# Moving the transposed input by 96 bytes in SBUF, in a two-layer hybrid encoder

## The chip, the cores and the metric

The kernel runs on one core of a Trainium2 chip. The metric is the device time of one execution in microseconds (us); before the change its median over three runs is 1843.59 us. The profile of one execution is read beside it. In it PE is TensorE's matmuls, PEld its weight loads (the loading of the stationary operand), DVE is VectorE, ACT ScalarE, POOL GpSimd, and SP the engine that issues most DMAs.

## What is computed

Two encoder layers over x of 512 tokens by 1024 channels, in float32. Each layer has three sub-layers, and each ends with `x = LayerNorm(ALPHA * x + f(x))`:

```python
proj = x @ w_in                       # queries, keys, values of A and B; u, v of C; gate logits
out_a = window_attention(aq, ak, av, a_sink)        # +-128 tokens, rotary, a sink logit per head
out_b = dense_block_attention(bq, bk, bv)           # all tokens, RMS-normed q and k, 2-D rotary
out_c = spatial_gating(u, v, c_ln_g, c_ln_b, c_ws, c_bs)
branches = jnp.stack([out_a, out_b, out_c], axis=2)
gates = jax.nn.sigmoid(gate + b_gate).reshape(B, S, N_BRANCH, D_MODEL)
h = (jnp.einsum('bsnc,ncd->bsnd', branches, w_branch) * gates).sum(axis=2) @ w_mix_out
...
h = memory_cross_attention(x, mem, x_wq, x_wkv, x_wo)   # 4 heads, 256 memory tokens
...
h = conv_ffn(x, f_w_up, f_conv_k, f_conv_b, f_w_down)   # 2 x 2816 channels, 3-tap convolution
```

## The kernel before

**Products in three parts.** Every float32 operand of a projection is kept as two float32r tiles, a high part (`split_hi`, on ACT) and the rest (`split_lo`, on DVE, in four cases on POOL). A product is three matmuls into the same PSUM bank, high by high, high by low and low by high: `mm3`, lines 137 to 140. The profile therefore shows most matmuls under L138, L139 and L140, and one 128-deep step of a product as one of each. In `nc.tensor.matmul(ps, lhsT=..., rhs=...)` `lhsT` is stationary (128 columns of 128 rows) and `rhs` moves (up to 512 columns).

**The transposed input.** `xT` (line 90) holds x transposed, as [128 partitions, 4 token tiles, high or low, 8 channel tiles, 128 tokens], 32 KB of each partition. It is written at the start from a transposed copy of the input (`split_xt`, line 1097), and three times a layer from TensorE transposes (`xT_step`, line 219, with `ident`; not at the end of the last layer). It is read in two forms:

- `proj_tm` (line 202): xT is stationary, one tile of 128 tokens, and a weight of 512 (keys and values: 256) contiguous columns moves. Used by `v_step`, `u_step`, `q_step` and `kv_step`.
- `proj_fm` (line 209): a weight is stationary and xT moves, four blocks of 128 tokens that lie 8 KB apart, or two of them (`hf`). Used by `gate_step`, `wq_step`, `up_step` and, in halves, `up_half_step`.

All other products have neither operand in xT: the branch projections (`br_step`), the mixer output (`mix_step`, operands `mh` and `ml`), the products with the memory (`mk_step`, `mv_step`, operand `memT`), attention, `wo_step` and the down projection (`down_mm`, operand `g`).

**Weights.** `Weights` (line 143) streams 292 chunks of 512 KB in the order in which the steps need them: a DMA on SP into one of two `raw` buffers, then a split into one of six `w` slots. A full step of the up projection uses one chunk in 8 x 3 = 24 matmuls of 512 columns; a step of the down projection uses one chunk in 4 x 2 x 3 = 24.

**Order.** `layer` puts the steps of a layer into a list (from line 943 on): v and u, the queries with the spatial gating between them, keys and values, then the 16 units of attention A between the gates and projections of branch C, attention B between those of branch A, those of branch B, the mixer output, cross attention, the up projection (22 pairs of steps, the first four steps in halves of 256 tokens) and the down projection. TensorE executes in the order that the scheduler makes of this list.

**Memory.** Tiles come from pools that are laid out in the order of their creation, each tile rounded up to 32 bytes. `cpool` (line 78) is the first and holds, in this order, `xT`, `rope`, `btab`, `mask`, `ident`, `ident_r`, `pp`, `hbias` and `mhalf`. In the compiled kernel `xT` starts at byte 1152 of every partition, `ident` at 41600 and `ident_r` at 42112, each a multiple of 128. Behind `cpool` come `wpool` (first `raw` at 44640, first `w` at 52832), `big`, `kv_p` and `sp`; each tile of these four pools starts 96 bytes past a multiple of 128. `mhalf` is one column of -0.5, the exponent in `rstd_of` (line 197).

Of the kernel before, what the change touches and what calls it, by code (L numbers as in the profile page):

```python
# [10 lines left out]
F32 = mybir.dt.float32  # L11
# [5 lines left out]
P = 128  # L17
# [56 lines left out]
def encoder_kernel(ctx: ExitStack, tc: tile.TileContext, x_in, xt_in, mem_in, w_in, pp_in, ln_in, cln_in, ws_in, co_in, out):  # L74
# [3 lines left out]
    cpool = ctx.enter_context(tc.tile_pool(name="cpool", bufs=1))  # L78
# [8 lines left out]
    ps_t = ctx.enter_context(tc.tile_pool(name="ps_t", bufs=2, space=PSUM))  # L87

    X = {}
    xT = cpool.tile([P, NT, 2, KD, P], F32R, name="xT")  # L90
    dram = ctx.enter_context(tc.tile_pool(name="dram", bufs=1, space=bass.MemoryType.DRAM))
    x_keep = dram.tile([S, DM], F32, name="x_keep")
# [4 lines left out]
    ident_r = cpool.tile([P, P], F32R, name="ident_r")  # L97
    pp = cpool.tile([P, PP_N], F32, name="pp")
    hbias = cpool.tile([P, 24], F32, name="hbias")
    mhalf = cpool.tile([P, 1], F32, name="mhalf")  # L100

    def acc_tile(n=512):
        return ps_acc.tile([P, 512], F32, tag="acc", name="acc")
# [16 lines left out]
    def sm(n, name):  # L120
        return small.tile([P, n], F32, tag=name, name=name)
# [17 lines left out]
        nc.tensor.matmul(ps, lhsT=lh, rhs=rl, start=False, stop=False)  # L139
        nc.tensor.matmul(ps, lhsT=ll, rhs=rh, start=False, stop=last)  # L140

# [1 line left out]
    class Weights:  # L143
        def __init__(self):
            self.order, self.pos, self.last = [], {}, []
# [47 lines left out]
    def pump():  # L193
        W.pump(cur[0])

# [1 line left out]
    def rstd_of(var, n, name):  # L197
        r = sm(n, name)
        nc.gpsimd.tensor_tensor(out=r, in0=var, in1=mhalf.to_broadcast([P, n]), op=ALU.pow)  # L199
        return r  # L200
# [14 lines left out]
    def evac_T(dst_h, dst_l, ps):  # L215
        split_hi(dst_h, ps)
        split_lo(dst_l, ps, dst_h)

    def xT_step(t):
        def fn():  # L220
            for i in range(2):
                pt = t_tile()
                for j in range(4):
                    k = 4 * i + j
                    nc.tensor.transpose(pt[:, j, :], X[0][:, t, k * P:(k + 1) * P], ident)
                evac_T(xT[:, t, 0, 4 * i:4 * i + 4, :], xT[:, t, 1, 4 * i:4 * i + 4, :], pt)
# [5 lines left out]
    def residual(t, half, ps):  # L232
        xs = X[0][:, t, half * 512:(half + 1) * 512]
        nc.vector.scalar_tensor_tensor(out=xs, in0=xs, scalar=ALPHA, in1=ps, op0=ALU.mult, op1=ALU.add)  # L234
        if half == 0:
            ln_stats[t] = small.tile([P, 2, 6], F32, tag="bn", name="bn", bufs=4)
        nc.vector.bn_stats(out=ln_stats[t][:, half, :], in_=xs)

    def ln_finish(t, g, b):
# [6 lines left out]
        for hf in range(2):  # L246
            xt = X[0][:, t, hf * 512:hf * 512 + 512]
            nc.vector.scalar_tensor_tensor(out=xt, in0=xt, scalar=mv[:, 0:1], in1=g[hf], op0=ALU.subtract, op1=ALU.mult)
        for hf in range(2):
            xt = X[0][:, t, hf * 512:hf * 512 + 512]  # L250
            nc.vector.scalar_tensor_tensor(out=xt, in0=xt, scalar=rs, in1=b[hf], op0=ALU.mult, op1=ALU.add)
# [11 lines left out]
        return tiles  # L263

    def rope_rot(t1, t2, src, cos, sin, nh, w):
        # rotate-half within blocks of 2*w, on nh heads of 64
        nb = 64 // (2 * w)
        s4 = src.rearrange("p h (b s d) -> p h b s d", b=nb, s=2)
        o4 = t2.rearrange("p h (b s d) -> p h b s d", b=nb, s=2)
        n4 = sin.rearrange("p (b s d) -> p b s d", b=nb, s=2)  # L270
        nc.vector.tensor_tensor(out=t1, in0=src, in1=cos[:, None, :].to_broadcast([P, nh, 64]), op=ALU.mult)
        for s in range(2):
            if nb == 1:
                nc.vector.tensor_tensor(out=o4[:, :, 0, s, :], in0=s4[:, :, 0, 1 - s, :],
                                        in1=n4[:, 0, s, :][:, None, :].to_broadcast([P, nh, w]), op=ALU.mult)
            else:
                nc.vector.tensor_tensor(out=o4[:, :, :, s, :], in0=s4[:, :, :, 1 - s, :],
                                        in1=n4[:, :, s, :][:, None, :, :].to_broadcast([P, nh, nb, w]), op=ALU.mult)
# [6 lines left out]
    def layer(l):  # L285
        K = lambda kind, c: (l, kind, c)
        R = {}
        last_layer = l == NLAYER - 1

# [1 line left out]
        def params():  # L291
            dma = nc.sync if l == 0 else nc.scalar
            dma.dma_start(out=pp, in_=pp_in[l])
            act(hbias, pp[:, PP_GATE:PP_GATE + 24], AF.Copy, scale=0.5)
            cl = kv_p.tile([P, 2, 512], F32, tag="k", name="cln")
            dma.dma_start(out=cl[:, 0, :], in_=cln_in[l, 0].partition_broadcast(P))
            dma.dma_start(out=cl[:, 1, :], in_=cln_in[l, 1].partition_broadcast(P))
            R["cln"] = cl
            wr = p_tile(name="wsraw")
            dma.dma_start(out=wr, in_=ws_in[l])  # L300
            ws = kv_p.tile([P, 2, 4, P], F32R, tag="v", name="ws", bufs=2)
            wr3 = wr.rearrange("p (g i) -> p g i", g=4)
            split_hi(ws[:, 0], wr3)
            split_lo(ws[:, 1], wr3, ws[:, 0])
            R["ws"] = ws
            R["vc"] = big_tile([P, 2, NT, 512], F32R, "vc")
            R["u"] = big_tile([P, NT, 512], F32, "u")
# [9 lines left out]
                nc.gpsimd.tensor_tensor(out=btab[:, i], in0=b4[:, i % 2],  # L317
                                        in1=g[:, None, :].to_broadcast([P, NT, 64]), op=ALU.mult)

# [1 line left out]
        def v_step(t):  # L321
            def fn():
                ps = acc_tile()
# [47 lines left out]
                pump()  # L371
            return Step(fn)

# [1 line left out]
        def q_step(nm, t):  # L375
            chunks = [K(nm + "q", c) for c in range(4)]

# [22 lines left out]
        def rms(src, tmp, nh):  # L400
            act(tmp, src, AF.Square)
            ss = sm(nh, "ss%d" % nh)
            nc.vector.tensor_reduce(out=ss, in_=tmp, axis=AX.X, op=ALU.add)
            nc.vector.tensor_scalar(out=ss, in0=ss, scalar1=1.0 / 64, scalar2=RMS_EPS, op0=ALU.mult, op1=ALU.add)
# [59 lines left out]
                pump()  # L464
            return Step(fn)

# [1 line left out]
        def a_keys(q):  # L468
            return max(0, q - 1), min(NT - 1, q + 1)

# [82 lines left out]
                evac_pv("A", h, ps)  # L553
            return Step(fn, urgent=True)

# [1 line left out]
        def bS_step(u):  # L557
            def fn():
                h, pr = u // 2, u % 2
# [3 lines left out]
                for qi in range(2):  # L563
                    q = 2 * pr + qi
                    ps = s_tile()
                    for hl in range(2):
                        nc.tensor.matmul(ps, lhsT=R["Q"][:, h, q * P:(q + 1) * P], rhs=R["Kt"][:, kv * 2 + hl, :],  # L567
                                         start=hl == 0, stop=hl == 1)
                    nc.vector.tensor_reduce(out=nm[:, qi:qi + 1], in_=ps, axis=AX.X, op=ALU.max, negate=True)  # L569
                    pm = pm_slot(2 * u + qi)  # L570
# [37 lines left out]
                    evac_pv("B", h, R.pop("pv"))  # L608
            return Step(fn, urgent=True)

# [1 line left out]
        def ring():  # L612
            if "ring" not in R:
                R["ring"] = big_tile([P, 8, 512], F32, "ring")
            return R["ring"]

        def pm_slot(i):
            return ring()[:, i % 4, :]
# [55 lines left out]
                f.append(br_step(n, m, stage))  # L674
            return f

# [1 line left out]
        def mix_step(half, t):  # L678
            chunks = [K("mix", half * 4 + c) for c in range(4)]

# [12 lines left out]
                    ln_finish(t, *R["ln"])  # L693
            return Step(fn, chunks)

# [1 line left out]
        def memT_step():  # L697
            def fn():
                R["memT"] = big_tile([P, 2, KD, NMEM], F32R, "memT")
# [138 lines left out]
                ln_finish(t, *R["ln"])  # L838
            return Step(fn, chunks)

# [1 line left out]
        def g_slot(j):  # L842
            if j % 4 == 0 and j < 20:
                R["g", j // 4] = big_tile([P, 4, 2, S], F32R, "g")
            elif j == 20:
                R["g", 5] = kv_p.tile([P, 2, 2, S], F32R, tag="k", name="g5")
            return g_view(j)
# [92 lines left out]
                        nc.sync.dma_start(out=out[t * P:(t + 1) * P, sl], in_=X[0][:, t, sl])  # L940
            return Step(fn, [K("down", 11 + c) for c in cs])

# [1 line left out]
        def st(s):  # L944
            steps.append(s)

# [139 lines left out]
    for l in range(NLAYER):  # L1086
        layer(l)
# [37 lines left out]
            W.pump(i)  # L1125


# [1 line left out]
def _pack_weights(d):  # L1129
    out = np.empty((NLAYER * NCH, P, 1024), np.float32)  # L1130

    def tm(w, c0, n, nk):
        # (K, n) columns c0.. cut in chunks of nk k-tiles: [p, k, n]
        kt = w.shape[0] // P
        a = w[:, c0:c0 + n].reshape(kt // nk, nk, P, n).transpose(0, 2, 1, 3)
        return a.reshape(kt // nk, P, nk * n)

    def fm(w):
        # (K, M) as [m, p, k, 128]
        kt, mt = w.shape[0] // P, w.shape[1] // P  # L1140
        return w.reshape(kt, P, mt, P).transpose(2, 1, 0, 3).reshape(mt, P, kt * P)

    for l in range(NLAYER):
        def put(kind, a):
            i = l * NCH + CHUNK_ID[kind, 0]
            out[i:i + a.shape[0]] = a

        w = d["w_in"][l]
        put("aq", tm(w, 0, 512, 2))
        put("akv", tm(w, 512, 256, 4))  # L1150
        put("bq", tm(w, 768, 512, 2))
        put("bkv", tm(w, 1280, 256, 4))
        put("u", tm(w, 1536, 512, 2))
        put("v", tm(w, 2048, 512, 2))
        put("gate", fm(w[:, 2560:]))
        put("br", np.concatenate([fm(d["w_branch"][l, n]).reshape(4, 2, P, 512).transpose(0, 2, 1, 3).reshape(4, P, 1024)
                                  for n in range(3)]))
        w = d["w_mix_out"][l]
        put("mix", np.concatenate([tm(w, 0, 512, 2), tm(w, 512, 512, 2)]))
        put("wq", fm(d["x_wq"][l]))  # L1160
        w = d["x_wkv"][l]
        put("mk", fm(w[:, :512]))
        put("mv", tm(w, 512, 512, 2))
        w = d["x_wo"][l]
        put("wo", np.concatenate([tm(w, 0, 512, 2), tm(w, 512, 512, 2)]))
        put("up", fm(d["f_w_up"][l]))
        w = d["f_w_down"][l]
        put("down", np.concatenate([tm(w, 0, 512, 2), tm(w, 512, 512, 2)]))
    return out
# [65 lines left out]
```

## Time and profile before

| what | value |
|---|---|
| median of three runs (lowest, highest) | 1843.59 us (1843.54, 1844.64) |
| span of the profiled execution | 1842.8 us |
| mean granted TensorE clock in it | 0.994 of full speed |
| matmuls in the trace | 9064 |

The span runs from the first to the last instruction of the profiled execution; the runs' median is 0.8 us longer. The page lists busy time by engine, the chain of work that ended last, and the costliest groups of instructions. A group's row gives line, engine, operation, out<-in with the moving operand first for matmuls, partitions by elements, the count, then busy time and the mean duration of one. Matmuls overlap each other: one starts before the last one has ended, so the mean duration of one is longer than the distance between two starts. A few matmul records are missing from the trace.

### The profile page before, as it was taken

The page shows a single profiled execution, that of the slowest core. Times are in us where ns is not written, and L with a number is a line of the kernel's source. Part 1 is how long each engine was busy: PE and PEld are TensorE (multiplying, and loading weights), DVE is VectorE, ACT ScalarE, POOL GpSimd, SP SyncE. Part 2 cuts the span into 40 slices and gives each one's busy share as a digit, 9 for nine tenths or more (in the row PEclk, how much of TensorE's full clock was granted, in tenths as well). Part 3 has the DMA queues.
Part 4 walks back from the last instruction along what each step waited for, and adds up shares of the span by engine and source line. Part 5 has one row for each costly group of instructions (what it writes and reads, how often), then busy time and mean ns, then how long its engine had stood idle before and what let it go on. Part 6 is the DMA issues. An engine that isn't in the chain of part 4 may idle for free.

```text
span 1842.8 us, 23541 instructions
## 1 busy us (share of the span) xinstructions
PE 1811.5 (98%) x9064; PEld 1516.5 (82%) x9064; DVE 1065.9 (58%) x1728; ACT 756.0 (41%) x1274; POOL 316.4 (17%) x320
## 2 busy tenths in 40 slices
PE   8999999999999999999999999999999999999998
PEld 6888888878978888888888888888789788888886
DVE  5566856557675555533466568565575755555334
ACT  4346635532534443331133565455325244444210
POOL 1112422220131111100011124331201311111000
PEclk9999999999999999999999999999999999999999
DMA  6221221232413222232233212212333222222321
GB/s 221 88 78 65 81 92 58 71 132 95 150 69 103 92 92 92 99 119 92 92 131 105 79 70 83 79 58 81 129 109 130 81 92 92 92 102 92 103 103 46
DMA packets 51233, 176.60 MB, mean 96 GB/s; under 512 B 5681, under 2 KB 6193, under 8 KB 50865
## 3 DMA queue, kind: packets, MB, share of 16 engines
q1 hardware_dynamic: 44784, 158.86, 24.8%
q10 hardware_dynamic: 6336, 16.23, 2.7%
q8 instruction: 72, 1.18, 0.3%
q14 instruction: 41, 0.33, 0.1%
HBM read 170.87 MB, written 4.19 MB: 95 GB/s over the span
## 4 chain that ended last, share of the span: by engine, by line
PE 97%; DVE 1%; ACT 1%; DMA 0%; issue 0%; DVEq 0%; SPq 0%
PE acc L138 26%; PE acc L139 26%; PE acc L140 26%; PE s L567 2%; PE pv L604 1%; PE t L590 1%; PE s L138 1%; PE s L140 1%; PE s L139 1%; PE t L140 1%; PE t L138 1%; PE t L139 1%; PE pv L139 1%; PE pv L549 1%; PE s L483 1%; PE pv L138 1%
## 5 line engine op out<-in xcount | busy, mean ns | idle before, releaser
L132 DVE TENSOR_TENSOR w<-raw,w 128x1024 fp32r<-128x1024 f32 x284 | 354.8, 1250 | 454.0 <-ACT w L127 452.9
L127 ACT ACTIVATE w<-raw 128x1024 fp32r<-128x1024 f32 x292 | 309.4, 1060 | 495.7 <-PE acc L140 276.7
L138 PE MATMUL acc<-xT,w 128*128 128x512 f32 (+1 forms) x1216 | 463.3, 382 | 4.5 <-DVE x L234 4.2
L140 PE MATMUL acc<-xT,w 128*128 128x512 f32 (+1 forms) x1216 | 464.5, 382 | 0.0
L139 PE MATMUL acc<-xT,w 128*128 128x512 f32 (+1 forms) x1216 | 462.6, 381 | 0.0
L138 PEld LDWEIGHTS acc<-xT,w 128*128 128x128 f32 x1216 | 228.4, 188 | 50.1 <-DVE x L234 4.6
L140 PEld LDWEIGHTS acc<-xT,w 128*128 128x128 f32 x1216 | 229.2, 189 | 45.8
L139 PEld LDWEIGHTS acc<-xT,w 128*128 128x128 f32 x1216 | 229.3, 189 | 45.5
L138 PE MATMUL acc<-w,xT 128*128 128x512 f32 (+1 forms) x384 | 138.2, 362 | 7.4 <-ACT w L127 7.2
L139 PE MATMUL acc<-w,xT 128*128 128x512 f32 (+1 forms) x384 | 138.6, 361 | 1.2 <-DVE w L132 1.2
L140 PE MATMUL acc<-w,xT 128*128 128x512 f32 (+1 forms) x384 | 138.4, 360 | 0.0
L870 POOL TENSOR_TENSOR cv<-cv 128x512 f32<-128x512 f32 x44 | 56.8, 1292 | 445.4 <-DVE cv L858 402.2
L199 POOL TENSOR_TENSOR rs<-ve,mhalf 128x1 f32<-128x1 f32 x32 | 30.2, 942 | 422.4 <-DVE ve L244 371.4
L138 PEld LDWEIGHTS acc<-w,xT 128*128 128x128 f32 x384 | 72.8, 189 | 18.9 <-ACT w L127 7.8
L139 PEld LDWEIGHTS acc<-w,xT 128*128 128x128 f32 x384 | 72.6, 189 | 13.5 <-DVE w L132 2.0
L140 PEld LDWEIGHTS acc<-w,xT 128*128 128x128 f32 x384 | 72.7, 189 | 10.8
L502 POOL TENSOR_SCALAR ring<-ring,rsm 128x256 f32<-128x256 f32 (+1 forms) x64 | 43.6, 693 | 186.2 <-DVE rsm L500 108.3
L569 DVE TENSOR_REDUCE nm<-s 128x1 f32<-128x512 f32 x64 | 43.9, 688 | 54.2 <-PE s L567 53.5
L124 ACT ACTIVATE ring<-s,nm 128x512 f32<-128x512 f32 x64 | 44.0, 688 | 69.7 <-PE t L590 45.4
L655 POOL TENSOR_TENSOR mg<-mg,ring 128x512 f32<-128x512 f32 x32 | 47.8, 1498 | 140.4 <-DVE ring L654 112.4
L576 POOL TENSOR_SCALAR ring<-ring,rsm 128x512 f32<-128x512 f32 x64 | 45.7, 727 | 129.7 <-DVE rsm L574 129.7
L124 ACT ACTIVATE cv<-acc,pp 128x512 f32<-128x512 f32 x86 | 65.4, 760 | 1.5 <-PE acc L140 1.5
(237 smaller groups left out, 3302.7 us busy)
## 6 DMA issues: line engine op xcount, KB each, us to landing
raw<-in_w_dram SPq DMA_DIRECT2D x292, 512.0 KB, 3.5
lngb<-in_ln_dram ACTq DMA_DIRECT2D x16, 256.0 KB, 4.3
xraw<-in_xt_dram SPq DMA_DIRECT2D x4, 512.0 KB, 4.7
memr<-in_mem_dram ACTq DMA_DIRECT2D x2, 1024.0 KB, 4.8
x<-in_x_dram ACTq DMA_DIRECT2D x4, 512.0 KB, 7.3
x_keep<-x ACTq DMA_DIRECT2D x4, 512.0 KB, 2.6
x<-x_keep ACTq DMA_DIRECT2D x4, 512.0 KB, 7.5
out_dram<-x SPq DMA_DIRECT2D x8, 256.0 KB, 2.0
```

The lines of the kernel that those rows point to most:

```text
L124: return nc.scalar.activation(out, in_, func, **kw)
L127: nc.scalar.activation(out, in_, AF.Copy, scale=scale)
L132: eng.tensor_tensor(out=out, in0=in_, in1=hi.bitcast(F32), op=ALU.subtract)
L138: nc.tensor.matmul(ps, lhsT=lh, rhs=rh, start=first, stop=False)
L139: nc.tensor.matmul(ps, lhsT=lh, rhs=rl, start=False, stop=False)
L140: nc.tensor.matmul(ps, lhsT=ll, rhs=rh, start=False, stop=last)
L502: nc.gpsimd.tensor_scalar(out=pr_t[qi], in0=pr_t[qi], scalar1=rs[:, qi:qi + 1], scalar2=0.0, op0=ALU.mult, op1=ALU.add)
L567: nc.tensor.matmul(ps, lhsT=R["Q"][:, h, q * P:(q + 1) * P], rhs=R["Kt"][:, kv * 2 + hl, :], start=hl == 0, stop=hl == 1)
L569: nc.vector.tensor_reduce(out=nm[:, qi:qi + 1], in_=ps, axis=AX.X, op=ALU.max, negate=True)
L576: nc.gpsimd.tensor_scalar(out=pr_t[qi], in0=pr_t[qi], scalar1=rs[:, qi:qi + 1], scalar2=0.0, op0=ALU.mult, op1=ALU.add)
L655: nc.gpsimd.tensor_tensor(out=mg, in0=mg, in1=tg, op=ALU.add)
L870: nc.gpsimd.tensor_tensor(out=c, in0=ca, in1=c, op=ALU.mult)
```

## The change

A tile `lead` of 24 floats (96 bytes) is put ahead of `xT` in `cpool`. `mhalf` is no longer a tile, but the first column of `lead`. Behind `hbias`, where `mhalf` was, stands a tile of 16 floats (64 bytes) that nothing uses.

```diff
     X = {}
+    lead = cpool.tile([P, 24], F32, name="lead")
     xT = cpool.tile([P, NT, 2, KD, P], F32R, name="xT")
...
     hbias = cpool.tile([P, 24], F32, name="hbias")
-    mhalf = cpool.tile([P, 1], F32, name="mhalf")
+    mhalf = lead[:, 0:1]
+    cpool.tile([P, 16], F32, name="tail")
```

The rest of the diff takes out comment lines. All tiles of `cpool` from `xT` to `hbias` lie 96 bytes further, and everything behind `cpool` 96 + 64 - 32 = 128 bytes further.

## The prediction

> **What bounds the kernel now.** I read the page's span and busy time first, then the chain that ended last, then PE's waits.
>
> ```profile
> span 1842.8 us, 23541 instructions
> ...
> PE 1811.5 (98%) x9064; PEld 1516.5 (82%) x9064; DVE 1065.9 (58%) x1728; ACT 756.0 (41%) x1274; POOL 316.4 (17%) x320
> ...
> PE 97%; DVE 1%; ACT 1%; DMA 0%; issue 0%; DVEq 0%; SPq 0%
> ```
>
> TensorE is busy for 98% of the span and 97% of the last chain is on it. Its longest single wait is at the start:
>
> ```profile
> PE acc L138 <- ACT w L127: 7.2, 1, 7.2
> PE acc L138 <- DVE x L234: 4.9, 4, 2.1
> ```
>
> So the time is, nearly, the number of matmuls times the distance from one matmul's start to the next. Only a shorter distance can make the kernel faster. The next question is whether that distance differs between operands. I read the groups by line with shapes kept apart, where an entry reads out<-moving,stationary.
>
> ```profile
> L140 PE MATMUL acc<-xT,w 128*128 128x512 f32 x1056 | 419.0, 397 | 0.0
> ...
> L138 PE MATMUL acc<-w,xT 128*128 128x512 f32 x256 | 101.8, 400 | 7.4 <-ACT w L127 7.2
> L140 PE MATMUL acc<-w,g 128*128 128x512 f32 x132 | 51.4, 389 | 0.0
> ...
> L138 PE MATMUL acc<-w,mh 128*128 128x512 f32 x128 | 50.0, 390 | 0.0
> ```
>
> Each of these is one of the three lines of `mm3`. Matmuls of 512 columns with xT as either operand last 397 to 400 ns, those of the down projection (`g`) and of the mixer output (`mh`) 389 to 390. The entries `w,xT` and `w,g` are the same form: a contiguous weight moves, 128 contiguous columns are stationary, the output is a PSUM bank. What differs in the instruction is where the stationary operand lies. Matmuls overlap, so a duration is not the distance. For that I count them in stretches without idle time (columns: stretch, its length, PE busy with count, clock, DMA share, GB/s). The first and third are in the up projection (xT moves), the others in the down projection.
>
> ```profile
> 600.00:800.00 200.00, 200.00 (x859) 1.00 0.27 94
> 830.00:910.00 80.00, 80.00 (x355) 1.00 0.27 93
> 1515.00:1715.00 200.00, 200.00 (x858) 1.00 0.27 95
> 1745.00:1825.00 80.00, 80.00 (x355) 1.00 0.21 73
> ```
>
> A matmul is counted if it touches the stretch, so the stretch is longer by about one duration: 200.4/859 = 233.3 ns per matmul with xT, 80.4/355 = 226.5 ns without. The clock (1.00) and the DMA share (0.27 in three rows) are the same. xT as the stationary operand gives the same distance, here in layer 2's first projection, ten steps in 2.33 us:
>
> ```profile
> 955.73 0.40 PE L138 MATMUL acc<-w,xT 128*128 128x512 f32 x1
> ...
> 958.06 0.40 PE L139 MATMUL acc<-w,xT 128*128 128x512 f32 x1
> ```
>
> The memory map of the compiled kernel puts xT at byte 1152 of each partition (9 x 128, remainder 0) and `w`, every tile of `big`, `kv_p` and `sp` at remainder 96 within 128. Of TensorE's operands only xT, `ident` and `ident_r` have remainder 0. The slow distance goes with the operand that lies apart.
>
> **The change, part by part.** No instruction is added or taken away; only addresses move.
>
> *xT.* `lead` is 96 bytes, so xT starts at 1248: remainder 96, and 224 within 512. `mhalf`'s 32 bytes go and a `tail` of 64 comes, so every later pool moves by 128 (96+64-32): remainder 96 again, and 224 within 512. xT then stands to `w` within 512 bytes as `g` and `mh` do now. Does the form with xT moving in four blocks, 8 KB apart, also profit? The spatial gating has a four-block moving operand (`vc`) whose place agrees with its stationary one:
>
> ```profile
> L140 PE MATMUL pv<-vc,ws 128*128 128x512 f32 x8 | 3.2, 396 | 0.0
> L138 PE MATMUL pv<-vc,ws 128*128 128x512 f32 x8 | 3.1, 392 | 0.0
> L139 PE MATMUL pv<-vc,ws 128*128 128x512 f32 x8 | 3.1, 390 | 0.0
> ```
>
> These come in threes between other work, and two of three lines are already near 390; I take the four-block form to profit too. Matmuls of 512 columns with xT are 3 x 1056 + 3 x 256 = 3936. In stretches of their own stand the up projection (2 layers x 40 steps x 24 = 1920), v and u (384), the full steps of `wq` (96) and the gates of branch B (384): 2784, by 6.8 ns (233.3 - 226.5) each **18.9 us**. The other 1152 (the gates of C and A and the queries) stand between transposes and attention matmuls. What equal place is worth there is read from the groups in that part of layer 1 (80 to 372 us):
>
> ```profile
> L140 PE MATMUL acc<-xT,w 128*128 128x512 f32 x168 | 67.3, 401 | 0.0
> L138 PE MATMUL acc<-xT,w 128*128 128x512 f32 x168 | 67.1, 399 | 0.0
> L139 PE MATMUL acc<-xT,w 128*128 128x512 f32 x168 | 66.4, 395 | 0.0
> ...
> L139 PE MATMUL acc<-brA,w 128*128 128x512 f32 x32 | 12.7, 396 | 0.0
> L138 PE MATMUL acc<-brC,w 128*128 128x512 f32 x32 | 12.7, 396 | 0.0
> ...
> L139 PE MATMUL acc<-brC,w 128*128 128x512 f32 x32 | 12.6, 393 | 0.0
> L140 PE MATMUL acc<-brC,w 128*128 128x512 f32 x32 | 12.5, 392 | 0.0
> ```
>
> xT has 398.3 on the mean, `brC` (equal place) 393.7, and the one line shown of `brA` 396. I take 3.1 ns, near the middle of 2.3 and 4.6: 1152 x 3.1 = **3.6 us**.
>
> *xT with 256 columns* (keys and values, halves of `wq` and of the first up steps: 960 matmuls) speaks against the change. `memT` has the equal place and is the slower:
>
> ```profile
> 1382.30 0.28 PE L139 MATMUL acc<-memT,w 128*128 128x256 f32 x1
> ...
> 1385.66 0.28 PE L140 MATMUL acc<-memT,w 128*128 128x256 f32 x1
> 1385.78 0.28 PE L138 MATMUL acc<-xT,w 128*128 128x256 f32 x1
> ...
> 1388.49 0.28 PE L140 MATMUL acc<-xT,w 128*128 128x256 f32 x1
> ```
>
> 28 steps in 3.36 us are 120.0 ns, 23 steps in 2.71 us are 117.8. I take the nearest row, a **loss** of 960 x 2.2 = **2.1 us**. The other end is half of 226.5, or 113.2: a gain of 4.4 us.
>
> *ident and ident_r* move with xT. Every transpose in the trace uses one of them, so none shows the equal place:
>
> ```profile
> L590 PE MATMUL t<-ident,ring 128*128 128x128 f32 x256 | 46.4, 272 | 2.6 <-DVE PTb L132 2.6
> L414 PE MATMUL t<-ident_r,qs 128*128 128x128 f32 x128 | 13.2, 242 | 0.0
> ```
>
> By the transposes the code issues there are 672 with `ident` and 192 with `ident_r`. The one size that the trace shows for such an effect is 6.8 ns a matmul, so the bounds are 5.9 us either way. I take 0, for want of a row on either side.
>
> *Everything else* costs nothing: `mhalf` is now a slice, written once and read by the same 32 POOL instructions; `tail` is never touched; loads of `rope`, `mask`, `pp` and `ident` land 96 bytes further. They are issued once (`pp` once per layer) and wait behind nothing new in their queues; if one came late, its first reader would be a later step of DVE, ACT or PE.
>
> **What is late next.** A shorter distance asks for weights sooner: a chunk every 24 x 226.5 = 5.44 us in place of 5.60.
>
> ```profile
> 590.00:810.00 220.00, 220.00 (x946) 176.92 (x945) 115.62 (x138) 90.01 (x119) 25.81 (x20) 1.00 0.28 98
> ...
> raw<-in_w_dram SPq DMA_DIRECT2D x292, 512.0 KB, 3.5
> ```
>
> In the up projection DVE is busy for 53% and ACT for 41% of the stretch; 3% less time makes that 54% and 42%. A load lands in 3.5 us, and two `raw` buffers hide it. The down projection uses a chunk every 5.44 us already, with no idle time in its rows above. So I let nothing take the gain back.
>
> [...]
>
> **The sum.** 18.9 + 3.6 - 2.1 = 20.4 us off the span of 1842.8, giving 1822.4. The median of the runs, 1843.59, is 0.8 above this span; with it **1823.2 us**, 1.1% faster. All terms at their best: 3936 x 6.8 = 26.8, + 4.4 + 5.9 = 37.1, giving 1806.5. The likeliest case's own range is 1814 to 1831: the upper end if only the stretches of their own gain, and only two thirds of it (12.6), the lower if the attention part gains in full and `ident` helps a little.
>
> **The rivals.**
>
> *The place is not the cause* (12%). xT also lies in the lowest 34 KB; if that region sets the 233.3, or if the two operands' reads never meet and something that the rows don't show sets it, nothing moves: 1843.6. [...] Against it: `g`, `mh` and `w` lie in many regions relative to each other, and the down rows are all at 389.
>
> *Only the contiguous form gains* (4%). xT in four blocks stays at 233.3. Then only v, u and the queries gain, 384 x 6.8 + 384 x 3.1 = 3.8, less 2.1: 1841.9, within the bound. The 396 in the `vc` rows speaks for it, the 390 against.
>
> *Slower: `ident` leaves the better place* (4%). Transposes may now run at the good of two distances and lose 6.8 ns each: 5.9 us. With the loss at 256 columns that is 8.0 us; it ends slower where xT's 3936 matmuls gain under 2.0 ns each on the mean, and with no gain there it gives 1851.6. For it only the 256-column rows, where equal place is the slower.
>
> **How the numbers follow.** Forecast case 76%, a larger gain (below 1814) 4%, the rivals 12, 4 and 4%. A measurement of this kernel tells about 0.2% (3.7 us) from no change. Faster: 76 + 4 = 80%; within 0.2%: 12 + 4 = 16%; slower: 4%. The range, 1810 to 1838, holds the forecast case and most of the larger gain; of the unknown costs it leaves out the outermost 3.5 us below and the cases without a gain.
>
> **What would show it.** Right: the stretches of the up projection count about 885 matmuls in 200 us, not 859; the groups with xT at 512 columns fall from 397 and 400 to about 390; those with `g` and `mh` stay. Right on the loss: xT at 256 columns steps at 120 ns. Wrong: xT still at 397, or transposes longer than 272, or PE idle time beside `w` in the up projection.

## The result and the profile after

The changed kernel takes 1822.6 us (median of 4 runs, 1821.89 to 1822.94); the kernel before, run beside it, 1844.05 us (1843.54 to 1844.64). The ratio is 0.9882, with a 95% interval of 0.987 to 0.9894: 1.2% faster, where 1823.2 us was forecast.

The page of the changed kernel has the same instructions and a span shorter by 21.7 us. TensorE and the chain that ended last keep their shares, so TensorE still bounds the kernel:

```profile
span 1821.1 us, 23541 instructions
...
PE 1790.4 (98%) x9064; PEld 1518.5 (83%) x9064; DVE 1064.7 (58%) x1728; ACT 756.0 (42%) x1274; POOL 317.3 (17%) x320
...
PE 97%; DVE 1%; ACT 1%; DMA 0%; issue 0%; DVEq 0%; SPq 0%
```

The groups by line with shapes apart (the new lines push `mm3` to lines 140 to 142):

```profile
L142 PE MATMUL acc<-xT,w 128*128 128x512 f32 x1056 | 413.7, 392 | 0.0
...
L140 PE MATMUL acc<-w,xT 128*128 128x512 f32 x256 | 100.5, 395 | 7.2 <-ACT w L129 7.2
L142 PE MATMUL acc<-w,g 128*128 128x512 f32 x132 | 51.4, 389 | 0.0
...
L592 PE MATMUL t<-ident,ring 128*128 128x128 f32 x256 | 46.4, 272 | 2.5 <-DVE PTb L134 2.5
...
L416 PE MATMUL t<-ident_r,qs 128*128 128x128 f32 x128 | 13.4, 243 | 0.0
```

The groups with xT fall from 397 and 400 to 392 and 395 ns on the mean of the whole kernel, not quite to the 390 forecast; those with `g` stay at 389 and the transposes at 272 and 242 to 243. What is left above 389 belongs to the parts between other work: in the up projection alone, the three lines are at 389. In stretches of their own xT now keeps pace with `g` (stretch, length, PE busy and count, clock, DMA share, GB/s; the first and third row are mostly and wholly the up projection, the second is the down projection):

```profile
600.00:800.00 200.00, 200.00 (x884) 1.00 0.31 102
825.00:905.00 80.00, 80.00 (x354) 1.00 0.28 92
1500.00:1690.00 190.00, 190.00 (x840) 1.00 0.29 97
```

190.4/840 is 226.7 ns from start to start, where 233.3 stood before.

Both traces hold the same 9064 matmuls in the same order, so each distance from one start to the next can be subtracted from its counterpart. Summed by kind, the 21.7 us come out as:

| matmuls | count | gain, us |
|---|---|---|
| xT moving, 512 columns | 3168 | 17.9 |
| xT stationary, 512 columns | 768 | 4.0 |
| xT, 256 columns | 960 | -0.6 |
| all others | 4168 | 0.4 |

### The profile page after: what moved, and what is told of

It is laid out like the page before. It is cut to its first block, busy times and chain, and to the rows that moved or that the text cites. A ratio compares the mean times of both kernels' runs of the same rounds, so it can differ in the third digit from the quotient of the medians.

```text
span 1821.1 us, 23541 instructions
## 1 busy us (share of the span) xinstructions
PE 1790.4 (98%) x9064; PEld 1518.5 (83%) x9064; DVE 1064.7 (58%) x1728; ACT 756.0 (42%) x1274; POOL 317.3 (17%) x320
## 4 chain that ended last, share of the span: by engine, by line
PE 97%; DVE 1%; ACT 1%; DMA 0%; issue 0%; DVEq 0%; SPq 0%
PE acc L140 26%; PE acc L141 25%; PE acc L142 25%; PE s L569 2%; PE pv L606 1%; PE t L592 1%; PE s L142 1%; PE s L140 1%; PE s L141 1%; PE t L142 1%; PE t L141 1%; PE t L140 1%; PE pv L141 1%; PE pv L551 1%; PE s L485 1%; PE pv L140 1%
## 5 line engine op out<-in xcount | busy, mean ns | idle before, releaser
L140 PE MATMUL acc<-xT,w 128*128 128x512 f32 (+1 forms) x1216 | 457.7, 378 | 4.2 <-DVE x L236 4.2
L142 PE MATMUL acc<-xT,w 128*128 128x512 f32 (+1 forms) x1216 | 459.4, 378 | 0.0
L141 PE MATMUL acc<-xT,w 128*128 128x512 f32 (+1 forms) x1216 | 457.5, 377 | 0.0
L201 POOL TENSOR_TENSOR rs<-ve,lead 128x1 f32<-128x1 f32 x32 | 30.2, 943 | 422.7 <-DVE ve L246 371.2
```

What stands on the lines that cost most here:

```text
L140: nc.tensor.matmul(ps, lhsT=lh, rhs=rh, start=first, stop=False)
```

## The experiments

The theory was that the gain comes from xT's place relative to the other operand, within 128 bytes. ("Within n bytes" means that only the remainder of a start address divided by n counts.) The rivals were that another size counts (32, 64, 256 or 512 bytes), that a certain remainder is the good one, that the lowest region is slow, and that `ident` has a share. Below, "distance" is the remainder of xT's start within 256 bytes less that of `w`'s and of all tiles in `big`, `kv_p` and `sp`; it is 32 bytes before and 0 after. Times of one run stand beside 1843.6 to 1844.5 us of the kernel before in the same jobs.

**All operands at remainder 0 within 128.** The kernel before with a tile of 32 bytes behind `mhalf`:

```diff
     mhalf = cpool.tile([P, 1], F32, name="mhalf")
+    cpool.tile([P, 8], F32, name="tail")
```

> xT stays at byte 1152 (remainder 0 within 128) and everything behind cpool moves by 32 bytes to remainder 0 as well, so all operands of TensorE agree again, but at another remainder than in the changed kernel. Theory 'the same place counts, not which': 1822 to 1824 us, xT at 512 columns 389 to 391 ns in the up projection. Rival 'remainder 96 is the good one, or xT has to leave a multiple of 128': 1843 us or more, and the down projection's 389 ns rise to about 395. Rival 'the lowest region of the memory is slow': xT still 395 ns, about 1843 us.

Measured: 1821.47 us (4 runs, 1821.19 to 1821.53), ratio 0.9875 (0.9859 to 0.9892). In the up projection xT lasts 389 ns:

```profile
L141 PE MATMUL acc<-xT,w 128*128 128x512 f32 x266 | 103.5, 389 | 0.0
```

xT has not moved at all. So neither its region nor a good remainder explains the 233 ns; what counts is that the two operands agree. One unused tile at the end of `cpool` does what the change does.

**Other distances: 64 short, 32 short, 128, and 256.** The changed kernel with other sizes of `lead` and `tail`:

```diff
-    lead = cpool.tile([P, 24], F32, name="lead")
+    lead = cpool.tile([P, 8], F32, name="lead")     # e2; 16 in e3; 24 in e4 and e5
...
-    cpool.tile([P, 16], F32, name="tail")
+    cpool.tile([P, 32], F32, name="tail")           # e2; 24 in e3; 48 in e4; 80 in e5
```

> xT, ident and ident_r at remainder 32, all else at 96: they differ by 64 bytes. Theory 'the place within 128 bytes has to agree': slow, 1840 to 1847 us, xT at 512 columns about 395 ns in the up projection. Rival 'the place within 64 (or 32) bytes has to agree': fast, 1822 to 1824 us and 389 ns.

> xT, ident and ident_r at remainder 64, all else at 96: xT lies 32 bytes short of the others, where before it lay 32 past them (0 against 96 is 96 short or 32 past). Theory 'any place that disagrees within 128 costs': 1840 to 1847 us, about 395 ns. Rival 'xT only has to leave the multiple of 128': 1822 to 1824 us and 389 ns.

> All operands at remainder 96 within 128, but xT at 224 and the others at 352 within 512: they disagree within 256 bytes. Theory 'the place within 128 counts': as the changed kernel, 1822 to 1824 us, 389 ns. Rival 'the place within 256 or 512 counts': 1840 us or more, about 395 ns.

> xT at 224 and all behind cpool at 480 within 512: they agree within 256 bytes and disagree within 512. Theory 'the place within 256 counts': as the changed kernel, 1822 to 1824 us, xT at 512 columns 389 ns in the up projection. Rival 'the place within 512 counts': 1835 to 1845 us, 393 to 396 ns.

Measured: 1841.5, 1844.68, 1841.13 and 1822.69 us. The first two are slow. That rules out sizes of 64 and 32 bytes, and that xT only has to leave the multiple of 128; the last two decide between 128 and more. At a distance of 128 bytes the kernel is slow although xT is "at the same place within 128 bytes". At 256 it is as fast as the changed kernel. Counts of the same stretch of the up projection, 128 bytes (first) and 256 bytes (second):

```profile
600.00:780.00 180.00, 180.00 (x776) 1.00 0.29 94
```

```profile
600.00:780.00 180.00, 180.00 (x796) 1.00 0.29 98
```

180.4/776 is 232.5 ns, 180.4/796 is 226.6. So the size within which the operands have to agree is, in this kernel, **256 bytes** (1841.13 us at a distance of 128, 1822.69 at 256). The change has a distance of 0 within 256 because its `tail` moves the later pools by 128 together with xT's move from 0 to 96; with 192 bytes in place of 64 it would have kept its description and lost all but some 3 us of its gain.

**xT alone, `ident` alone.** In the first, 32 bytes stand ahead of `ident` and `tail` is 32 bytes shorter, so that `ident` and `ident_r` are again 32 bytes past the others. In the second, the kernel before gets 480 bytes ahead of `ident` and 32 behind `mhalf`: `ident` agrees, xT does not.

```diff
+    cpool.tile([P, 8], F32, name="pad")             # e6; 120 in e7
     ident = cpool.tile([P, P], F32, name="ident")
```

> xT as in the changed kernel; ident and ident_r put back 32 bytes past the place of the others, as they were before. Theory 'all of the gain is xT's': 1822 to 1823.5 us, transposes 272 and 242 ns as in both kernels. Rival 'ident has a share': 1826 us or more, or less than 1820.

> xT stays 32 bytes past the place of the others; ident and ident_r get the equal place. Theory 'all of the gain is xT's': 1843 to 1845 us. Rival 'ident has a share': 1840 us or less, or over 1847.

Measured: 1821.89 us (4 runs, 1821.42 to 1822.8; ratio 0.9876, 0.9859 to 0.9892) and 1845.91 us (one run). The second is 0.9 us above the range that the theory gave, which is less than these runs can tell. The transposes, first with `ident` 32 bytes off and then with it in place, are equal:

```profile
L593 PE MATMUL t<-ident,ring 128*128 128x128 f32 x256 | 46.4, 272 | 2.6 <-DVE PTb L135 2.6
...
L417 PE MATMUL t<-ident_r,qs 128*128 128x128 f32 x128 | 13.4, 243 | 0.0
```

```profile
L592 PE MATMUL t<-ident,ring 128*128 128x128 f32 x256 | 46.4, 272 | 2.5 <-DVE PTb L134 2.5
...
L416 PE MATMUL t<-ident_r,qs 128*128 128x128 f32 x128 | 13.3, 243 | 0.0
```

All of the gain is xT's.

**16 bytes past and 16 short.** xT is cut from a tile 32 bytes longer, from its fifth element on; `tail` is 32 bytes in e9, `lead` 64 bytes in e10.

```diff
-    xT = cpool.tile([P, NT, 2, KD, P], F32R, name="xT")
+    xT = cpool.tile([P, NT * 2 * KD * P + 8], F32R, name="xT")[:, 4:4 + NT * 2 * KD * P].rearrange(
+        "p (t s k c) -> p t s k c", t=NT, s=2, k=KD)
```

> xT 16 bytes past the place of the others within 256 (ident 32 past, as it was before). Theory 'the place has to agree to the byte': slow, 1838 to 1846 us, xT at 512 columns 393 to 396 ns in the up projection. Rival 'it has to agree in pieces of 32 bytes' (224 and 240 lie in the same one): as the changed kernel, 1821 to 1824 us, 389 ns.

> xT 16 bytes short of the place of the others, 208 against 224, in the piece of 32 bytes before. Theory 'to the byte' and rival 'in pieces of 32 bytes' both say slow: 1838 to 1846 us, 393 to 396 ns. If it is fast here and 16 bytes past, then 16 bytes are too little to matter.

Measured: 1837.23 and 1843.53 us, the first a little below its 1838. Neither side of the theory came out whole, because the two forms part. 16 bytes past, xT moving in the up projection and xT stationary in layer 2's v:

```profile
L143 PE MATMUL acc<-xT,w 128*128 128x512 f32 x260 | 102.5, 394 | 0.0
```

```profile
L142 PE MATMUL acc<-w,xT 128*128 128x512 f32 x28 | 10.9, 389 | 0.0
```

16 bytes short it is 400 (in layer 2's up projection 396) and 390 to 391. So 16 bytes are enough to cost where xT moves, and cost 2 ns at most where a contiguous weight moves against a stationary xT. Smaller distances were not tried.

**The other products out of place.** The changed kernel with 32 bytes between `wpool` and `big`:

```diff
+    shift = ctx.enter_context(tc.tile_pool(name="shift", bufs=1))
     big = ctx.enter_context(tc.tile_pool(name="big", bufs=6))
...
+    shift.tile([P, 8], F32, name="shift")
```

> The changed kernel with big, kv_p, sp and small moved by 32 bytes against w and xT, so that the products with xT keep the equal place and the products of w with g, mh, ml, oT, memT and the branch outputs lose it. Theory 'the place of the two operands within 256, whichever they are': 1728 matmuls in stretches of their own x 6.6 = 11.4 us, 576 of the branch projections x 3 to 6.6 = 1.8 to 3.8 us more than the changed kernel: 1835 to 1839 us, the down projection's 389 ns become 395, xT stays at 389. Rival 'it is something about xT or its region': 1822 to 1824 us, g at 389.

Measured: 1835.93 us. The rows are exchanged: xT in the up projection, then `g`:

```profile
L142 PE MATMUL acc<-xT,w 128*128 128x512 f32 x266 | 103.5, 389 | 0.0
```

```profile
L143 PE MATMUL acc<-w,g 128*128 128x512 f32 x132 | 52.2, 396 | 0.0
```

So it is the pair of operands that pays, not xT: the products of `w` with `g`, `mh` and `ml` now last 395 to 398 ns, and the 13.3 us over the changed kernel lie inside the 13.2 to 15.2 worked out beforehand. The products of 256 columns are exchanged as well, and the other way: those with `memT`, now out of place, get faster. In the changed kernel (first) and in this run:

```profile
L141 PE MATMUL acc<-memT,w 128*128 128x256 f32 x64 | 18.3, 285 | 0.0
```

```profile
L143 PE MATMUL acc<-memT,w 128*128 128x256 f32 x64 | 18.1, 282 | 0.0
```

**Which two operands have to agree.** xT becomes two tiles with 32 bytes between them; the high half is in place, the low half 32 bytes past it. In the second run the last two lines of `mm3` also change places.

```diff
-    xT = cpool.tile([P, NT, 2, KD, P], F32R, name="xT")
+    xT_hi = cpool.tile([P, NT, KD, P], F32R, name="xT_hi")
+    cpool.tile([P, 8], F32, name="pad")
+    xT_lo = cpool.tile([P, NT, KD, P], F32R, name="xT_lo")
...
-        nc.tensor.matmul(ps, lhsT=lh, rhs=rl, start=False, stop=False)
-        nc.tensor.matmul(ps, lhsT=ll, rhs=rh, start=False, stop=last)
+        nc.tensor.matmul(ps, lhsT=ll, rhs=rh, start=False, stop=False)     # e12 only
+        nc.tensor.matmul(ps, lhsT=lh, rhs=rl, start=False, stop=last)      # e12 only
```

> xT is made of two tiles, the high half at the place of the others, the low half (and ident) 32 bytes past it; one matmul in three of each product has the low half. Theory 'each matmul pays for its own pair of operands or for its neighbour's load': a third of the loss comes back, 0.33 x 3936 x 6.6 = 8.7 us, giving 1830 to 1833 us, with one of the three lines about 6 to 7 ns slower than the other two or the loss spread over two of them. Rival 'one operand out of place keeps the whole stream at the slow distance': 1841 to 1845 us, all three lines at about 395 ns in the up projection.

> As the run with the low half out of place, but each product's second and third matmul change places (high by high, low by high, high by low in mm3's names of stationary by moving). There the slowest start-to-start distance was the second line's in both forms: where xT is moving (237 ns, this matmul moves the low half) and where xT is stationary (239 ns, the low half is loaded while it runs, for the next one). Theory 'what counts is the operand that moves against the load that runs beside it, the next matmul's': the slowest becomes the third line where xT moves, and the first line where xT is stationary. Rival 'the matmul's own pair counts': the third line where xT moves, the second where xT is stationary. Rival 'it is the position in the three': the second line in both. Time 1836 to 1840 us in all of them.

Measured: 1838.21 and 1836.77 us. The first lies between the two theories it was to decide. Of three matmuls two pay, not one and not all: from start to start the three lines of the first group below take 231 (L148), 237 (L149) and 226 ns (L150). First run, in the up projection of layer 2 (low half moves in L149) and in layer 2's v (low half stationary in L150):

```profile
L149 PE MATMUL acc<-xT_lo,w 128*128 128x512 f32 x246 | 97.7, 397 | 0.0
L148 PE MATMUL acc<-xT_hi,w 128*128 128x512 f32 x245 | 96.3, 393 | 0.0
L150 PE MATMUL acc<-xT_hi,w 128*128 128x512 f32 x246 | 95.4, 388 | 0.0
```

```profile
L149 PE MATMUL acc<-w,xT_hi 128*128 128x512 f32 x27 | 10.8, 399 | 0.0
L150 PE MATMUL acc<-w,xT_lo 128*128 128x512 f32 x27 | 10.5, 390 | 0.0
L148 PE MATMUL acc<-w,xT_hi 128*128 128x512 f32 x25 | 9.7, 394 | 0.0
```

With xT stationary, the matmul whose own operand is out of place (L150) is the fastest, and the slowest is the one that runs just before it. In the second run, the up projection of layer 1 and layer 2's v:

```profile
L150 PE MATMUL acc<-xT_lo,w 128*128 128x512 f32 x260 | 103.4, 398 | 0.0
L149 PE MATMUL acc<-xT_hi,w 128*128 128x512 f32 x261 | 102.7, 393 | 0.0
L148 PE MATMUL acc<-xT_hi,w 128*128 128x512 f32 x260 | 101.0, 388 | 0.0
```

```profile
L150 PE MATMUL acc<-w,xT_hi 128*128 128x512 f32 x27 | 10.7, 395 | 0.0
L149 PE MATMUL acc<-w,xT_lo 128*128 128x512 f32 x27 | 10.5, 390 | 0.0
L148 PE MATMUL acc<-w,xT_hi 128*128 128x512 f32 x25 | 10.0, 399 | 0.0
```

The slowest follows as the theory of the load beside it says: L150, which moves the low half, in the first group; in the second L148, during which the low half is loaded for L149. The own pair (L149) and the position in the three (the second, L149) are both out. So what fits both runs is that a matmul is slowest, 397 to 399 ns where the fastest of its three takes 388 to 390, when the operand that moves does not agree with the weights that are loaded **for the next matmul**, while it runs. In the kernel before, L139's weights are loaded from the start of the L138 ahead of it:

```profile
1500.35 0.39 PE L138 MATMUL acc<-xT,w 128*128 128x512 f32 x1
1500.35 0.19 PEld L139 LDWEIGHTS acc<-xT,w 128*128 128x128 f32 x1
...
1500.58 0.40 PE L139 MATMUL acc<-xT,w 128*128 128x512 f32 x1
```

Why these two have to agree is not shown. The line ahead of the slowest pays about 5 ns too (393 to 395 against 388 to 390); the theory does not say why. In the other layer of each run (up projection) the same line is the slowest, but the three lie within 3 ns of each other (392 to 395 in the first run, 393 to 395 in the second), so the sharing out isn't the same in every stretch.

## Why the prediction was right

**The bound.** Right: no instruction was removed, the shares of TensorE stayed, and the shorter distance was the whole gain.

**xT at 512 columns.** Forecast 18.9 + 3.6 = 22.5 us, measured 21.9. By stage, from the paired distances: up projection 12.8 (13.1 forecast), v, u and queries 4.0 (3.8), gates 4.8 (5.0), `wq` 0.3 (0.7). The four-block form gained in full, as read from the three `vc` rows. The 3.1 ns for the parts between other work were near: in 80 to 372 us the three groups went from 398.3 to 394.7 on the mean, and by the paired distances xT moving gained 3.8 ns there.

```profile
L142 PE MATMUL acc<-xT,w 128*128 128x512 f32 x168 | 66.8, 397 | 0.0
L140 PE MATMUL acc<-xT,w 128*128 128x512 f32 x168 | 66.4, 395 | 0.0
L141 PE MATMUL acc<-xT,w 128*128 128x512 f32 x168 | 65.8, 392 | 0.0
```

**xT at 256 columns.** The sign was right: 0.6 us lost, 2.1 forecast. The distance did become 120 ns, here 23 steps in 2.76 us:

```profile
1371.34 0.28 PE L140 MATMUL acc<-xT,w 128*128 128x256 f32 x1
...
1374.10 0.28 PE L142 MATMUL acc<-xT,w 128*128 128x256 f32 x1
```

The price of the place was nearly right, too. In both traces 871 of the 960 are followed by the next matmul within 126 ns; they step at 117.7 ns before and 119.7 after, a loss of 1.7 us. The other 89 gained 1.1 us, mostly by the clock. At the first halves of the up projection the granted clock is 0.50 for a few us, and a matmul of 256 columns then steps at 213 ns. In layer 2 this lasted 6.8 us before and 3.4 us after, which gave 1.2 us back. In the run with xT alone (e6) xT and `w` lie at the same bytes as in the changed kernel, and the matmuls of the first halves that the rows list under `pv` last 320, 320 and 307 ns where the changed kernel has 332, 335 and 320: what these lose does not follow the place alone. Here are the kernel before and then the changed one (columns as above):

```profile
1463.50:1469.50 6.00, 6.00 (x28) 0.50 0.24 84
```

```profile
1449.50:1452.50 3.00, 3.00 (x16) 0.50 0.02 5
1452.50:1455.50 3.00, 3.00 (x26) 0.96 0.51 173
```

In layer 1 it covered more of these matmuls after than before and took 0.4 us. So it is luck that 0.6 us were lost and not 1.7. Little of it is left in the whole: the changed kernel has one more such stretch, from 374.1 to 377.5 us, in which the products with `brB` lose 0.7 us. The span fell by 21.7 us where 20.4 were forecast: 0.6 less at 512 columns, 1.5 more at 256, and 0.4 from the others.

**The transposes.** 0 was taken, with bounds of 5.9 us either way for want of a row. Their rows are the same in the runs with xT alone and `ident` alone, so 0 holds. The rival "`ident` leaves the better place" falls with that.

**What is late next.** Nothing, as forecast: the longest waits of TensorE are the same (7.2 us at the start; four on `x`, 4.8 us together where it was 4.9; two on `brB`, 4.1).

**What did not hold.** The reason was stated as the remainder within 128, with agreement within 512 beside it. Only the second was sufficient: within 128 alone, the forecast would have been 1823 for e4, which took 1841. The change meets both, which the prediction had worked out; by the first reason alone it would have been right by luck. The rivals "the place is not the cause" and "the lowest region" fall with the kernel that leaves xT where it was (1821.47 us). Whether the two operands' reads meet, of which the first rival speaks, no run shows. The runs do show that with xT moving 32 to 128 bytes out of place a matmul of 512 columns takes 6 to 7 ns longer from start to start (232.5 to 233.4 against 226.6), and the two runs with the low half out of place put the highest price where the next weights are loaded.

## What to carry to other kernels

Where TensorE bounds a kernel of float32r matmuls of 512 columns that each load new weights, try giving all its operands the same start within 256 bytes: in this kernel that took xT's from 395 ns to 389 in the up projection (at 256 columns the same start was 2 ns slower); an unused tile of 32 bytes behind the constants was enough here (1821.47 us). To see whether it pays, compare the start-to-start distance of groups with the same shape and different operands: 227 against 233 ns was the whole finding here. Check the agreement in the compiled memory map, since tiles whose size is no multiple of 256 bytes (here `pp`, `hbias` and `mhalf`) shift everything behind them.

## What was not expected of the hardware

Distances of xT and what they cost, with the mean duration of one matmul in the up projection of layer 1 and in layer 2's v:

| distance within 256, bytes | time, us | xT moving, ns | xT stationary, ns |
|---|---|---|---|
| 0 (all at remainder 0 within 128) | 1821.5 | 389 | 389 |
| 0 (e5, 256 apart) | 1822.7 | 389 | 389 |
| 16 past | 1837.2 | 394 | 389 |
| 16 short | 1843.5 | 400 (396 in layer 2) | 390 |
| 32 past (before) | 1844.1 | 395 | 396 |
| 32 short | 1844.7 | 396 | 395 |
| 64 short | 1841.5 | 394 | 391 (389 to 393 by line) |
| 128 | 1841.1 | 395 | 395 |

It is not a price that grows with the distance: any of the tried distances costs 5 to 11 ns where xT moves. With 16 bytes, and less with 64, the two forms part, which nothing here explains. At 256 columns the equal place is the slower, 120.0 against 117.8 ns in an undisturbed stretch, and the run with the other products out of place shows the same from the other side (`memT`, 285 and 282 ns). Whether at 512 columns some distance that wasn't tried beats 0 stays open, as does why the size is 256 bytes.
